# Low parts of streamed weight blocks on VectorE alone, in a two-layer decoder step with expert retrieval

## The chip, the cores and the metric

One core of a Trainium2 chip. Times are device microseconds of one execution of the whole program. PE is TensorE (PEld its weight loads), DVE is VectorE, ACT is ScalarE, POOL is GpSimd, SP is the engine that issues most DMAs here. L141 is line 141 of the kernel.

## What is computed

Two layers of a decoder for one prompt of 512 tokens and 8 sample sequences of 8 tokens: 576 tokens of 1024 channels, all in float32. A layer has a mixer (a gated linear recurrence and a short convolution) and then an expert retrieval, which is where the change lies:

```python
q = (xb @ w_q).reshape(tb, PEER_HEADS, 2, D_KEY_HALF)
s = jnp.einsum('thpd,hpkd->thpk', q, sub_keys).astype(jnp.float32)
sv, si = lax.top_k(s, TOPK)
cand = sv[:, :, 0, :, None] + sv[:, :, 1, None, :]
...
fv, fi = lax.top_k(cand, TOPK)
idx = jnp.take_along_axis(cand_idx, fi, axis=-1)
g = jax.nn.softmax(fv, axis=-1)
ue = u_tab[idx]
act = jax.nn.gelu(jnp.einsum('thkd,td->thk', ue, xb).astype(jnp.float32), approximate=False)
ve = v_tab[idx]
return jnp.einsum('thk,thkd->td', (g * act).astype(xb.dtype), ve)
```

8 heads choose 16 of 16384 experts for each token. An expert has a row of `u_tab`, whose product with the token is its activation, and a row of `v_tab`, which is added with weight gate times activation.

## The kernel before

**Two ways to the experts.** 384 tokens (TD) meet all 16384 experts on PE, 128 experts (a block) at a time; a gate matrix that is zero except at the chosen experts masks the result. For the other 192 tokens (three groups of 64, two partitions to a token) the chosen rows are gathered: 192 times a layer an indirect DMA, issued by GpSimd, brings one row of `u_tab` to each of 128 partitions (tile `ur`, L520), and VectorE forms the dot product with the token (L526); then 192 times a row of `v_tab` (`vr`, L520), which VectorE adds into `acc` (L541 the first time, L543 after). Between the two stand one Gelu over all dots and their product with the gates (`weigh`, L531). Five gathered tiles can be in flight (ROWS).

**Products in three passes.** Every streamed weight block [128, 1024] comes as `raw` (SP, L149; six in flight, RAWS) and is split in `split_blk` into `hi`, a rounded copy by ScalarE (L140), and `lo = raw - hi` (L141), a subtraction by VectorE or GpSimd; of each four can be in flight (HIS). PE multiplies hi with the high and the low part of the tokens, and lo with the high part. `turn` and `pool_share` say which engine makes lo: share 0 always VectorE (mixer), 0.5 every other block, 1.0 always GpSimd.

**The stages of the retrieval** of one layer:
- `queries`: 16 blocks of w_q (share 0.5), products pq (L722), scores, the 16 best of each half (`topk_half`, L586 to L591, on VectorE) and for the gathered tokens the choice of experts (`combine`, L601 to L661) and the dot steps as soon as their numbers are there.
- `dense_slots`: `combine` for the 384 tokens, four PE transposes (ptd, L771) for each 128.
- `phase_a`: 48 halves of gate pieces, each of two comparisons `oh` (L794) and two products `A` (L800) on VectorE, products pgm on PE (L805), a copy `stg` by ScalarE (L807) and, for two halves, a DMA to DRAM (gd, L809). Beside them the activations of the first 80 blocks of u: split (share SHARE_A = 1.0), product `pu` (L512, 24 matmuls a block), Gelu (L830).
- `phase_b`: for all 128 blocks the gates come back (gt, L886), activation times gate (L900), its split into wh and wl (L902, L903), the block of v (share SHARE_B = 0.5) and 18 matmuls `pvo` (L870). The last 48 blocks of u (names with `ub`, share SHARE_B) are multiplied here too, shortly before their v. pvo needs all gate pieces.

**What sets the order.** Nothing is ordered by hand. The program is written stage by stage, with the gathered steps strewn in by `pump` at rates QRATE, ARATE and BPUMP; a scheduler with a model of the engines' times then merges the instructions into one queue for each engine, by priority and by what it takes to be ready. Splits and loads of streamed blocks have a priority 2000 ahead (AHEAD). Each engine runs its queue strictly in that order.

Of the kernel before, what the change touches and what calls it, by code (L numbers as in the profile page):

```python
# [20 lines left out]
P = 128  # L21
L = 2              # layers
D = 1024
KT = D // P        # channel tiles
NP = 512           # prompt tokens
SB, ST = 8, 8      # sample sequences, steps
NS = SB * ST
T = NP + NS        # all tokens, prompt first
HA = 256           # the products over all tokens go by two parts, split here
# [4 lines left out]
TD = 384           # tokens that meet every expert on the tensor engine  # L34
NT = TD // P
NG = (T - TD) // 64  # groups of 64 tokens whose experts are gathered
NA = 80            # expert blocks that meet the tokens while the gates are formed
NS_ = NA - 16       # of these, the ones whose activations wait in DRAM
GI = 8             # expert blocks per reload
NCH = TD // 16     # 16-token pieces of the gate matrix  # L40
EPS = 1e-6
NEG = -3.0e38
GS = 16384.0       # keeps both float16 parts of a gate out of the subnormals
# [3 lines left out]
ROWSETS = [(0, 1), (1, 2), (2, 3), (3, 4), (4, 5), (5, 8), (8, 16)]  # rows of one length  # L47
AHEAD = 2000       # how far the streamed weights are put before the rest
NB = 4             # modulation chunks of the second layer that wait until the second norm of the first
NOW = 0            # the scheduler's rank of what the gathers and gates wait for  # L50
TROW = 1           # the pair of query blocks after which the gathered tokens' rows are formed
PACE = 0.8         # part of the first activations during which the gates are formed
TCOL = [0, 128, 384]    # tokens that meet every expert: first of each 128
GCOL = [256, 320, 512]  # tokens whose experts are gathered: first of each 64
NAT = 18           # gate pieces up to which every other one is formed where later activations stay
ONPE = (0, 256)    # tokens from these columns on have their squares summed on the tensor engine
SQ = 4             # pairs of blocks before the end at which the square root's table comes
WB = 2             # weighted activations in flight
X1, X2, X3 = 2, 3, 5   # modulation chunks before the load of x, its squares and its norm
EARLY = 20000      # how far the first loads are put before the rest  # L60
BOTH = 5           # modulation chunks in flight at the start
UAHEAD = 1         # pairs of blocks whose activations run ahead of their products
RAWS, HIS = 6, 4   # blocks of streamed weights in flight, as they come and split
ROWS = 5           # gathered rows in flight
SHARE_A, SHARE_B = 1.0, 0.5   # of the splits, what GpSimd takes
QRATE, ARATE, BPUMP = 0.3, 0.5, 1.6   # gathers issued beside queries, gates and products

# columns of the packed vectors
# [4 lines left out]
def hybrid_step(ctx: ExitStack, tc: tile.TileContext, xT, cT, wada, vecs, fnorm, win, wout, wq, subk,  # L73
# [18 lines left out]
    # ---------------------------------------------------------------- constants  # L92
# [25 lines left out]
    # conditioning vectors, one column quarter of the tensor engine wide, and the matrix that sums the four quarters  # L118
# [8 lines left out]
    # ---------------------------------------------------------------- helpers  # L127
    turn = [0.0]

    def split_blk(raw, nm, pool_share=0.0):  # L130
        """raw = hi + lo, both exact in float32r"""
        hi = st.tile([P, D], F32R, tag="hi", bufs=HIS, name=f"hi_{nm}")
        lo = st.tile([P, D], F32R, tag="lo", bufs=HIS, name=f"lo_{nm}")
        turn[0] += pool_share
        e = V
        if turn[0] >= 1.0:
            turn[0] -= 1.0
            e = G
        with tc.high_priority(offset=AHEAD):
            S.activation(hi, raw, AF.Copy)  # L140
            e.tensor_tensor(out=lo, in0=raw, in1=hi.bitcast(F32), op=ALU.subtract)  # L141
        return hi, lo

    def load_pair(src, nm, ahead=AHEAD):
        """two blocks of a stream, [P, D] each"""
# [6 lines left out]
    def mm_tokens(out, hi, lo, xh, xl, halves=((0, 1),)):  # L152
        """out[m, token] over all tokens, float32 from three passes"""
# [11 lines left out]
    def whole(o):  # L165
        """all tokens of a product in two banks"""
        return o.rearrange("p q t -> p (q t)")[:, 512 - HA:512 + HB]

# [4 lines left out]
    def ada(l, chunks, pool=None):  # L173
        """mod[p, part * 8 + k, sequence], 256 columns to a chunk. Four channel tiles at once go through the tensor
        engine, each in a column quarter of its own"""
# [23 lines left out]
    def bring(l, ch, n, ms):  # L199
        """n chunks' way to the partitions, with the bias"""  # L200
# [8 lines left out]
    def settle():  # L209
        """what was put off behind other work: the last chunk's way to the partitions, the last sums of the samples"""  # L210
        while late:
            late.pop()()

    def squares(pool, tag, k, c0, c1, nm):
        """ss += the squares of channel tile k"""
# [7 lines left out]
    def all_squares(c0, n, sq):  # L223
        """the squares of all channel tiles for n tokens, summed when rstd asks for them"""
# [8 lines left out]
    def rstd(c0, c1, nm):  # L233
        """ss = 1 / sqrt(mean square + eps)"""
# [12 lines left out]
    def norm_mod(pool, mod, nrm, part, nm, put, put_samples, ranges, tag=("nt", 2), ready=False):  # L247
        """modulate(rmsnorm(x)): shift at mod part, scale at part + 1. The prompt goes to put without the shift,
        channel tile by channel tile, the samples go whole and complete to put_samples"""
# [27 lines left out]
    def split_shift(hi, lo, tmp, shift):  # L277
        """tmp + shift = hi + lo"""
# [7 lines left out]
    def decay_rates():  # L286
        """-8 softplus(-lambda) and half of its size, the log1p by its atanh series"""
# [19 lines left out]
    # ---------------------------------------------------------------- mixer  # L307
    def mixer(l, vt, mod):
        with tc.tile_pool(name=f"hn{l}", bufs=1) as hn, tc.tile_pool(name=f"mh{l}", bufs=1) as mh:
# [6 lines left out]
            # output projection and residual  # L316
            g1 = mod[:, 2 * KT:3 * KT, :]
            for pr in range(KT // 2):
# [4 lines left out]
                # the last two by parts, so that the norm of the first part runs beside the second  # L323
# [18 lines left out]
    def mixer_in(l, vt, mod, mx, hnh, hnl, mgh, mgl):  # L342
# [25 lines left out]
        for c in range(KT):  # L368
# [22 lines left out]
            # recurrent branch: xa, its convolution, the gates, the scan  # L391
# [52 lines left out]
            # gated short convolution  # L444
# [34 lines left out]
    # ---------------------------------------------------------------- expert retrieval  # L479
    def peer(l, vt, mod):  # L480
# [4 lines left out]
        with tc.tile_pool(name=f"pg{l}", bufs=1) as pg:  # L485
            h2h = pg.tile([P, KT, TD], F32R, name="h2h")
            h2l = pg.tile([P, KT, TD], F32R, name="h2l")
            # slots of a gathered token: partition half r has heads 4 r + 0 .. 3
# [9 lines left out]
            def pump(n):  # L498
                """issue n more steps of the gathered tokens' work"""
# [16 lines left out]
            # tokens whose experts are gathered  # L516
# [67 lines left out]
    def topk_half(pool, sv, si, sc, nm, tick):  # L584
        """the 16 largest of the 128 scores and their places"""
# [8 lines left out]
    def combine(pool, sv4, si4, nh, nm, gate, ii, jj, tick, gscale=None, bufs=1):  # L594
        """the best 16 sums of each head: gates and both key numbers. Of the 256 sums (a, b) of the sorted halves
        only those with (a + 1)(b + 1) <= 16 can be among them; they lie row after row, row a from OFF[a] on"""
# [18 lines left out]
        # softmax over the 16  # L615
# [4 lines left out]
        # places: row a by comparison with the rows' starts, b = place - OFF[a]  # L620
# [12 lines left out]
        def rows(out):  # L633
            """out = the sums of pr's rows (integers up to 2048: exact)"""
# [28 lines left out]
    def queries(l, vt, mod, pg, pq, h2h, h2l, svd, sid, gidx, gate, xt, udot, gtasks, pump):  # L663
        """second norm, queries, scores, the best 16 keys of each half, and the gathered tokens' experts"""
# [28 lines left out]
        def token_rows():  # L693
            """the gathered tokens' vectors, token on the partition, in both halves"""
# [11 lines left out]
        for m in range(8):  # L706
# [6 lines left out]
            for u in range(2):  # L713
                hp = m + 8 * u
                hi, lo = split_blk(raw[u], f"wq{l}_{hp}", 0.5)
# [42 lines left out]
    def dense_slots(l, pk, svd, sid, sl, pump):  # L758
        """the chosen experts of the dense tokens, slots on the partition: both key numbers and the gate in two parts"""
# [14 lines left out]
    def phase_a(l, pg, pc, pa, sl, gd, ad, u_mm, pump):  # L774
        """gates as matrices to DRAM, and the activations of the first experts"""
# [3 lines left out]
        def slot(t, a, c0):  # L779
            """row a of the slots' numbers and gates for 8 tokens, beside every key number"""  # L780
            return sl[t][:, a, c0:c0 + 8].rearrange("p (g n) -> p g n", n=2).unsqueeze(2).to_broadcast([P, 4, P, 2])

        def gate_piece(t, ch):
            # pieces on their way to DRAM, the first ones also where later activations stay
# [32 lines left out]
        for pr in range(NA // 2):  # L817
# [8 lines left out]
            for u in range(2):  # L826
                i = 2 * pr + u
                hi, lo = split_blk(raw[u], f"u{l}_{i}", SHARE_A)
# [15 lines left out]
    def phase_b(l, pg, pc, pb, g2, gd, ad, res, u_mm, pump, finish):  # L844
# [9 lines left out]
        def meet(pair):  # L854
            """the activations of two blocks that come only now"""
# [3 lines left out]
            for u in range(2):  # L859
                i = i0 + 2 * pr + u  # L860
                hi, lo = split_blk(uraw[u], f"ub{l}_{i}", SHARE_B)
# [14 lines left out]
        for n, (i0, pr) in enumerate(pairs):  # L876
# [3 lines left out]
            if n == P // 2 - SQ:  # L880
                # brings the function's table early
# [12 lines left out]
            for u in range(2):  # L894
                i = i0 + 2 * pr + u
                w = acts[(i0, pr)][:, u, :] if at is None else at[:, i - i0, :]
                vh, vl = split_blk(vraw[u], f"v{l}_{i}", SHARE_B)
# [35 lines left out]
    # ---------------------------------------------------------------- the step  # L933
# [37 lines left out]
def _chan(a):  # L971
    """(..., D) -> channel-major (128, 8, ...)"""
# [5 lines left out]
def _layout(i):  # L978
# [7 lines left out]

    def pm(v, lead=()):  # (L, D) -> (L, P, KT)
        return v.reshape(L, -1, P).transpose(0, 2, 1)
# [5 lines left out]
    # column blocks in the order in which the mixer takes them: xa, ga, gb, cg, xs, bg  # L994
# [4 lines left out]
    w = i["peer_w_q"].reshape(L, KT, P, 2, 8, P).transpose(0, 4, 2, 3, 1, 5)  # l m p u k n  # L999
    o["wq"] = f(w.reshape(L, 8, P, 2, D))  # L1000
    o["subk"] = f(i["peer_sub_keys"].reshape(L, 2, 8, P, P).transpose(0, 2, 4, 1, 3))  # l m d u key
# [39 lines left out]
```

## Time and profile before

| | us |
|---|---|
| runs shown | 3847.15, 3849.39, 3852.28 |
| their median | 3849.39 |
| profiled execution, span from first to last instruction | 3846.9 |
| PE busy | 3484.8 |
| DVE busy | 3204.7 |
| POOL busy | 2022.2 |
| ACT busy | 1476.0 |

The profiled execution has no time of its own in the list of runs; its span is 0.3 us below the fastest run and 2.5 us below the median, so what lies around the span is no more than some microseconds. Layer 0 takes the first 1967 us, of which the retrieval is about 517 to 1945; layer 1 repeats it some 1870 us later. Busy time of an engine that is not waited for costs nothing, so the stretches are to be read one by one. An instruction's duration on DVE holds also the time in which it is held up after it has begun.

### The profile page before, as it was taken

To read this page: it belongs to the slowest core of one execution; us is meant where nothing else is said; L and a number is where in the kernel's file an instruction comes from. 1 tells how busy PE (TensorE), PEld (TensorE's weight loads), DVE (VectorE), ACT (ScalarE), POOL (GpSimd) and SP (SyncE) were. 2 spreads that over 40 slices of the span, in tenths; PEclk is the share of its full clock that TensorE was granted. 3 is DMA by queue.
4 is the path that set the end of the run, shared out by engine and by line. 5 is a ranking of instruction groups with operands and counts; after the bars stand their busy time and mean duration, and the time that the engine had idled before them with its cause. 6 is when DMAs were issued, how large, how long until landed. Compare 5 with 4: busy or idle time off the path is not lost.

```text
span 3846.9 us, 57240 instructions
## 1 busy us (share of the span) xinstructions
PE 3484.8 (91%) x21120; PEld 3180.7 (83%) x21120; DVE 3204.7 (83%) x5485; ACT 1476.0 (38%) x1876; POOL 2022.2 (53%) x1360
## 2 busy tenths in 40 slices
PE   8999998776879999999989998987677899999997
PEld 6999988776768999888879998877676799998886
DVE  5444489999997999998875556999999879999888
ACT  4444332322554333333344543222245533333332
POOL 1000037677536788776620002566764568887664
PEclk9999999888979999999989999988898899999998
DMA  6555237776878999999832221677678799999995
GB/s 249 188 189 165 69 138 263 246 233 223 291 272 298 334 338 340 341 358 362 315 131 79 82 83 65 209 254 233 225 263 279 280 338 322 338 357 342 355 341 200
DMA packets 366712, 960.62 MB, mean 250 GB/s; under 512 B 45920, under 2 KB 149472, under 8 KB 359648
## 3 DMA queue, kind: packets, MB, share of 16 engines
q1 hardware_dynamic: 239712, 478.77, 36.8%
q0 software_dynamic: 110592, 402.70, 30.0%
q10 hardware_dynamic: 16128, 75.50, 5.1%
q8 instruction: 165, 2.70, 0.3%
q14 instruction: 115, 0.94, 0.1%
HBM read 878.51 MB, written 78.30 MB: 249 GB/s over the span
## 4 chain that ended last, share of the span: by engine, by line
PE 55%; DVE 36%; issue 4%; DMA 2%; POOL 2%; ACT 1%; SPq 0%; DVEq 0%; POOLq 0%; ACTq 0%
PE pvo L870 19%; PE pj L159 16%; PE pu L512 12%; DVE ur L526 11%; DVE oh L794 4%; DVE A L800 4%; PE po L159 3%; POOL vr L520 1%; PE pq L722 1%; PE pm L189 1%; POOL lo_v L141 1%; DVE acc L543 1%; PE pg L420 1%; DMA raw_v<-in_vtab_dram 1%; PE pt L203 1%
## 5 line engine op out<-in xcount | busy, mean ns | idle before, releaser
L520 POOL DMA_INDIRECT ur<-in_utab_dram,gidx x384 | 481.6, 1254 | 512.9 <-DVE dot L526 281.2
L520 POOL DMA_INDIRECT vr<-in_vtab_dram,gidx x384 | 540.8, 1408 | 250.5 <-DVE acc L543 173.4
L543 DVE SCALAR_TENSOR_TENSOR acc<-vr,dot,acc 128x1024 f32<-128x1024 f32 x378 | 644.6, 1705 | 10.6 <-DMA vr<-in_vtab_dram,gidx 7.2
L526 DVE CUSTOM_DVE_ANT_0 ur<-ur,xt 128x1024 f32<-128x1024 f32 x384 | 613.4, 1605 | 8.8 <-DMA ur<-in_utab_dram,gidx 8.8
L512 PE MATMUL pu<-h2h,hi_u 128*128 128x384 f32 x1280 | 454.0, 355 | 62.4 <-ACT ao L830 62.4
L870 PE MATMUL pvo<-hi_v,wh 128*128 128x512 f32 x1536 | 488.7, 392 | 0.0
L870 PE MATMUL pvo<-lo_v,wh 128*128 128x512 f32 x1536 | 477.6, 390 | 0.0
L870 PE MATMUL pvo<-hi_v,wl 128*128 128x512 f32 x1536 | 466.0, 390 | 2.4 <-DVE acc L543 1.2
L512 PE MATMUL pu<-h2h,lo_u 128*128 128x384 f32 x1280 | 452.5, 353 | 6.0 <-POOL lo_u L141 5.9
L512 PE MATMUL pu<-h2l,hi_u 128*128 128x384 f32 x1280 | 451.2, 352 | 0.0
L141 POOL TENSOR_TENSOR lo_u<-raw_u,hi_u 128x1024 fp32r<-128x1024 f32 x160 | 405.6, 2537 | 28.5 <-ACT hi_u L140 25.7
L141 POOL TENSOR_TENSOR lo_v<-raw_v,hi_v 128x1024 fp32r<-128x1024 f32 x128 | 343.8, 2686 | 65.4 <-ACT hi_v L140 63.0
L159 PE MATMUL pj<-hnl,hi_wi 128*128 128x256 f32 (+1 forms) x1536 | 343.1, 301 | 2.5 <-DVE hnl L280 2.4
L159 PE MATMUL pj<-hnh,hi_wi 128*128 128x256 f32 (+1 forms) x1536 | 339.7, 301 | 5.5 <-ACT hnh L283 4.1
L870 PEld LDWEIGHTS pvo<-hi_v,wl 128*128 128x128 f32 x1536 | 288.1, 188 | 64.2 <-DVE wl L903 1.6
L870 PEld LDWEIGHTS pvo<-lo_v,wh 128*128 128x128 f32 x1536 | 288.3, 188 | 61.3
L159 PE MATMUL pj<-hnh,lo_wi 128*128 128x256 f32 (+1 forms) x1536 | 337.7, 298 | 0.0
L870 PEld LDWEIGHTS pvo<-hi_v,wh 128*128 128x128 f32 x1536 | 285.3, 188 | 54.9 <-issue 0.4
L512 PEld LDWEIGHTS pu<-h2h,hi_u 128*128 128x128 f32 x1280 | 256.4, 200 | 65.6 <-ACT ao L830 64.9
L140 ACT ACTIVATE hi_u<-raw_u 128x1024 fp32r<-128x1024 f32 x160 | 169.7, 1061 | 317.0 <-PE pu L512 162.4
L140 ACT ACTIVATE hi_v<-raw_v 128x1024 fp32r<-128x1024 f32 x256 | 272.0, 1062 | 29.5 <-issue 13.8
L512 PEld LDWEIGHTS pu<-h2h,lo_u 128*128 128x128 f32 x1280 | 255.9, 200 | 17.9 <-POOL lo_u L141 13.8
(319 smaller groups left out, 7592.8 us busy)
## 6 DMA issues: line engine op xcount, KB each, us to landing
raw_v<-in_vtab_dram SPq DMA_DIRECT2D x256, 512.0 KB
raw_u<-in_uT_dram SPq DMA_DIRECT2D x160, 512.0 KB
raw_wi<-in_win_dram SPq DMA_DIRECT2D x96, 512.0 KB
gd<-stg ACTq DMA_DIRECT2D x48, 1024.0 KB
raw_ub<-in_uT_dram SPq DMA_DIRECT2D x96, 512.0 KB
gt<-gd SPq DMA_DIRECT2D x768, 64.0 KB
raw_ada<-in_wada_dram SPq DMA_DIRECT2D x86, 512.0 KB
ad<-ao ACTq DMA_DIRECT2D x64, 384.0 KB
```

The costliest lines, as they stand in the source:

```text
L140: S.activation(hi, raw, AF.Copy)
L141: e.tensor_tensor(out=lo, in0=raw, in1=hi.bitcast(F32), op=ALU.subtract)
L159: PE.matmul(part(out, q), a[:, w], b[:, k, PARTS[q][0]:PARTS[q][1]], start=(k == 0 and a is hi and b is xh), stop=(k == KT - 1 and a is lo))
L189: PE.matmul(pm[j * 32:(j + 1) * 32, 0:256], c32[:, k, :], raw[k // 4][:, j * 256:(j + 1) * 256], start=(k < 4), stop=(k >= 4))
L203: PE.matmul(pt[:, q * 16:q * 16 + NSEQ], ms[:, q * P:(q + 1) * P], sel, start=True, stop=True)
L512: PE.matmul(pu[:, 0:TD], a[:, w], b[:, k, 0:TD], start=(k == 0 and a is hi and b is h2h), stop=(k == KT - 1 and a is lo))
L520: G.indirect_dma_start(out=rt, out_offset=None, in_=tab, in_offset=bass.IndirectOffsetOnAxis(ap=gidx[:, g, h, k:k + 1], axis=0))
L526: V.tensor_tensor_reduce(out=ur, in0=ur, in1=xt[g], scale=1.0, scalar=0.0, op0=ALU.mult, op1=ALU.add, accum_out=dot[:, g, h, k:k + 1])
L543: V.scalar_tensor_tensor(out=acc[g], in0=vr, scalar=w, in1=acc[g], op0=ALU.mult, op1=ALU.add)
L794: V.tensor_tensor(out=o, in0=iota2.unsqueeze(1).to_broadcast([P, 4, P, 2]), in1=slot(t, a, c0), op=ALU.is_equal)
L800: V.tensor_tensor(out=A[:, z], in0=oh[0], in1=slot(t, 2 + z, c0), op=ALU.mult)
L870: PE.matmul(pv[t][q], a[:, tk], b[:, q * 512:(q + 1) * 512], start=(n == 0 and a is wh and b is vh), stop=(n == P - 1 and a is wl))
```

## The change

GpSimd's share becomes 0 in all four places where blocks are split with a share: the 16 blocks of w_q, and the u and v blocks of phase_a and phase_b. `split_blk` itself stays. The rest of the diff drops comments.

```diff
-SHARE_A, SHARE_B = 1.0, 0.5   # of the splits, what GpSimd takes
+SHARE = 0.0
...
-                hi, lo = split_blk(raw[u], f"wq{l}_{hp}", 0.5)
+                hi, lo = split_blk(raw[u], f"wq{l}_{hp}", SHARE)
...
-                hi, lo = split_blk(raw[u], f"u{l}_{i}", SHARE_A)
+                hi, lo = split_blk(raw[u], f"u{l}_{i}", SHARE)
...
-                hi, lo = split_blk(uraw[u], f"ub{l}_{i}", SHARE_B)
+                hi, lo = split_blk(uraw[u], f"ub{l}_{i}", SHARE)
...
-                vh, vl = split_blk(vraw[u], f"v{l}_{i}", SHARE_B)
+                vh, vl = split_blk(vraw[u], f"v{l}_{i}", SHARE)
```

The scheduler makes other queues of it. Three places follow, before and after; numbers behind a name are block or step and a tile's number.

VectorE in `dense_slots` of layer 0, around the cast of the first gates (L766); before:

```order
L526 ISA ur_1_1_14_9148,dot_4954<-ur_1_1_14_9148,xt_1_5521 128x1024
L526 ISA dot_4954 128x1
L766 CAST ghd_0_7090<-ggd_0_7088 128x128
L637 TENSOR_TENSOR t8d_0_7170<-t8d_0_7170 128x128x2
L613 MAX_INDEX fid_1_7235<-fvd_1_7234,c2d_1_3_7259 128x8
L611 MATCH_REPLACE c2d_1_4_7265<-fvd_1_7234,candd_1_7226 128x50
```

and after:

```order
L141 TENSOR_TENSOR lo_u_62_10970<-raw_u_31_10964,hi_u_62_10969 128x1024
L526 ISA ur_1_2_0_11870,dot_4954<-ur_1_2_0_11870,xt_1_5521 128x1024
L526 ISA dot_4954 128x1
L766 CAST ghd_0_7090<-ggd_0_7088 128x128
L613 MAX_INDEX fid_1_7235<-fvd_1_7234,c2d_1_2_7253 128x8
L637 TENSOR_TENSOR t8d_0_7170<-t8d_0_7170 128x128x2
L141 TENSOR_TENSOR lo_u_63_11000<-raw_u_31_10965,hi_u_63_10999 128x1024
L613 MAX_INDEX fid_1_7235<-fvd_1_7234,c2d_1_3_7259 128x8
L526 ISA ur_1_2_1_11900,dot_4954<-ur_1_2_1_11900,xt_1_5521 128x1024
```

Subtractions have come into VectorE's queue, the block of u beside the same cast is 63, and the dot steps have gone on from the second to the third head of their group.

VectorE in the gate stage of layer 0; before:

```order
L794 TENSOR_TENSOR oh_1_32_9014<-iota_83,sl_1_4956 128x1024
L794 TENSOR_TENSOR oh_1_32_9016<-iota_83,sl_1_4956 128x1024
L800 TENSOR_TENSOR A_1_32_9021<-oh_1_32_9014,sl_1_4956 128x1024 x2
L526 ISA ur_1_2_10_12294,dot_4954<-ur_1_2_10_12294,xt_1_5521 128x1024
L526 ISA dot_4954 128x1
L794 TENSOR_TENSOR oh_1_40_9042<-iota_83,sl_1_4956 128x1024
L794 TENSOR_TENSOR oh_1_40_9047<-iota_83,sl_1_4956 128x1024
L800 TENSOR_TENSOR A_1_40_9049<-oh_1_40_9042,sl_1_4956 128x1024 x2
```

and after:

```order
L543 SCALAR_TENSOR_TENSOR acc_0_15106<-vr_0_2_3_15906,dot_4954,acc_0_15106 128x1024
L794 TENSOR_TENSOR oh_1_40_9047<-iota_83,sl_1_4956 128x1024
L800 TENSOR_TENSOR A_1_32_9021<-oh_1_32_9014,sl_1_4956 128x1024 x2
L543 SCALAR_TENSOR_TENSOR acc_0_15106<-vr_0_2_4_15936,dot_4954,acc_0_15106 128x1024
L794 TENSOR_TENSOR oh_1_40_9042<-iota_83,sl_1_4956 128x1024
L543 SCALAR_TENSOR_TENSOR acc_0_15106<-vr_0_2_5_15970,dot_4954,acc_0_15106 128x1024
L794 TENSOR_TENSOR oh_1_48_9143<-iota_83,sl_1_4956 128x1024
L800 TENSOR_TENSOR A_1_40_9049<-oh_1_40_9042,sl_1_4956 128x1024 x2
```

The gathered work beside the same gate products was the 43rd dot of the second group; now all dots are done and the sums of the first group run.

PE at the last gate product of layer 0 (pgm); before:

```order
L805 LDWEIGHTS oh_2_120_10938
L805 MATMUL pgm_2_7_1_10932<-A_2_120_10940,oh_2_120_10938 128x128
L512 MATMUL pu_73_11326<-h2l,hi_u_73_11322 128x384
L512 MATMUL pu_73_11326<-h2h,lo_u_73_11323 128x384
L512 MATMUL pu_73_11326<-h2h,hi_u_73_11322 128x384
```

and after:

```order
L805 LDWEIGHTS oh_2_120_10938
L805 MATMUL pgm_2_7_1_10932<-A_2_120_10940,oh_2_120_10938 128x128
L512 MATMUL pu_82_11626<-h2h,hi_ub_82_11622 128x384
L512 MATMUL pu_82_11626<-h2l,hi_ub_82_11622 128x384
L512 MATMUL pu_82_11626<-h2h,lo_ub_82_11623 128x384
```

In both the first pvo stands behind pu of block 85, or two matmuls into it, so PE has 283 matmuls of pu between the two before and 96 after.

## Rows read from the trace of the kernel before

**Rows 1.** The page: busy time of each engine, and the chain that ended last.

```profile
PE 3484.8 (91%) x21120; PEld 3180.7 (83%) x21120; DVE 3204.7 (83%) x5485; ACT 1476.0 (38%) x1876; POOL 2022.2 (53%) x1360
PE 55%; DVE 36%; issue 4%; DMA 2%; POOL 2%; ACT 1%; SPq 0%; DVEq 0%; POOLq 0%; ACTq 0%
```

**Rows 2.** Table by stretch: start:end, length, engines' busy time, granted clock, DMA share, GB/s.

```profile
core 0: us, PE busy (x) PEld busy (x) DVE busy (x) ACT busy (x) POOL busy (x), PEclk, DMA share, GB/s
517.00:1186.00 669.00, 527.11 (x3478) 497.85 (x3477) 655.38 (x1605) 247.83 (x273) 392.49 (x233) 0.88 0.72 243
1186.00:1945.00 759.00, 757.76 (x3672) 665.57 (x3670) 674.59 (x644) 285.49 (x378) 567.24 (x325) 1.00 0.95 338
...
960.00:1190.00 230.00, 176.88 (x1352) 159.08 (x1351) 229.24 (x289) 126.38 (x98) 116.32 (x71) 0.86 0.81 281
1335.00:1596.00 261.00, 261.00 (x1330) 238.57 (x1329) 248.94 (x201) 94.01 (x127) 215.29 (x122) 1.00 0.95 342
```

**Rows 3.** Tiles A (layer 0), ur, oh, lo_u, lo_wi: duration min/median/max, first and last start.

```profile
L800 DVE TENSOR_TENSOR A<-oh,sl x96: 675/682/3261, 968.0 to 1182.0; 128x1024 f16<-128x1024 f16 x96
L526 DVE CUSTOM_DVE_ANT_0 ur<-ur,xt x384: 1192/1212/4065, 569.7 to 3198.4; 128x1024 f32<-128x1024 f32 x192
L794 DVE TENSOR_TENSOR oh<-iota,sl x192: 674/681/5640, 960.0 to 3052.1; 128x1024 f16<-128x1024 f16 x192
L141 POOL TENSOR_TENSOR lo_u<-raw_u,hi_u x160: 2346/2407/4423, 618.9 to 3069.7; 128x1024 fp32r<-128x1024 f32 x160
L141 DVE TENSOR_TENSOR lo_wi<-raw_wi,hi_wi x96: 1197/1224/1226, 36.2 to 2274.9; 128x1024 fp32r<-128x1024 f32 x96
```

**Rows 4.** The chain that ended last: the gate stage (first line), then 1186 to 1345 us.

```profile
by line: DVE oh L794 33.9%; DVE A L800 31.0%; DVE ur L526 24.7%; PE pu L512 7.3%; PE pgm L805 2.0%; issue 1.3%; DVE dot L526 0.2%
by line: PE pu L512 63.3%; PE pvo L870 36.3%; PE pgm L805 0.6%; issue 0.0%
1186.88 49.14 PE pu L512 x283
...
1248.42 8.20 PE pvo L870 x36
1256.62 8.34 PE pu L512 x48
```

**Rows 5.** Groups of DVE, 517 to 1186 us: busy, mean ns, idle before, releasers.

```profile
L526 DVE CUSTOM_DVE_ANT_0 ur<-ur,xt 128x1024 f32<-128x1024 f32 x147 | 235.9, 1606 | 4.8 <-DMA ur<-in_utab_dram,gidx 4.8
L794 DVE TENSOR_TENSOR oh<-iota,sl 128x1024 f16<-128x1024 f16 x96 | 85.5, 921 | 0.3
L800 DVE TENSOR_TENSOR A<-oh,sl 128x1024 f16<-128x1024 f16 x96 | 82.6, 900 | 0.5
```

**Rows 6.** Timeline of DVE in three places: start, length, instruction.

```profile
1186.37 1.21 DVE L526 CUSTOM_DVE_ANT_0 ur<-ur,xt 128x1024 f32<-128x1024 f32 x1
1187.51 1.21 DVE L526 CUSTOM_DVE_ANT_0 ur<-ur,xt 128x1024 f32<-128x1024 f32 x1
1188.66 3.42 DVE L526 CUSTOM_DVE_ANT_0 ur<-ur,xt 128x1024 f32<-128x1024 f32 x1
...
1238.79 1.21 DVE L141 TENSOR_TENSOR lo_v<-raw_v,hi_v 128x1024 fp32r<-128x1024 f32 x1
1239.93 0.54 DVE L900 TENSOR_TENSOR ao<-ao,gt 128x384 f32<-128x384 f32 x1
...
1606.33 1.27 DVE L543 SCALAR_TENSOR_TENSOR acc<-vr,dot,acc 128x1024 f32<-128x1024 f32 x1
1607.53 1.21 DVE L141 TENSOR_TENSOR lo_v<-raw_v,hi_v 128x1024 fp32r<-128x1024 f32 x1
```

**Rows 7.** Groups of POOL, 517 to 1186 us.

```profile
L141 POOL TENSOR_TENSOR lo_u<-raw_u,hi_u 128x1024 fp32r<-128x1024 f32 x76 | 193.1, 2543 | 14.3 <-ACT hi_u L140 13.0
L141 POOL TENSOR_TENSOR lo_wq<-raw_wq,hi_wq 128x1024 fp32r<-128x1024 f32 x6 | 14.6, 2432 | 38.2 <-ACT hi_wq L140 38.2
```

**Rows 8.** Groups of DVE and POOL in the gate stage, 960 to 1190 us.

```profile
L526 DVE CUSTOM_DVE_ANT_0 ur<-ur,xt 128x1024 f32<-128x1024 f32 x49 | 74.0, 1515 | 0.0
L141 POOL TENSOR_TENSOR lo_u<-raw_u,hi_u 128x1024 fp32r<-128x1024 f32 x25 | 62.9, 2518 | 12.2 <-ACT hi_u L140 11.8
```

**Rows 9.** The page: the queue of the 768 gathers.

```profile
q0 software_dynamic: 110592, 402.70, 30.0%
```

**Rows 10.** Timeline of ACT, SP, DVE from A to B; of PE and DVE at layer 0's end.

```profile
1189.95 0.33 ACTq L809 DMA_DIRECT2D gd<-stg  x1
...
1206.23 4.62 SPq L886 DMA_DIRECT2D gt<-gd  x7
...
1233.07 3.71 DVE L900 TENSOR_TENSOR ao<-ao,gt 128x384 f32<-128x384 f32 x4 [2.38 <-DMA gt<-gd]
...
1944.34 1.03 PE L920 MATMUL pyt<-ident,ys 128*128 128x128 f32 x8
...
1961.16 1.19 DVE L543 SCALAR_TENSOR_TENSOR acc<-vr,dot,acc 128x1024 f32<-128x1024 f32 x1
```

## The prediction

> **What bounds the kernel now.** I read the page first, then its stages one by one. The page says that PE is busy 91% and DVE 83% of the span, and that the chain that ended last is 55% PE and 36% DVE [rows 1]: two different bounds, so the next view is the table by stretch, here for the expert retrieval of the first layer (the second layer repeats it). From 517 to 1186 us DVE is busy 655 of 669 us while PE works 527; from 1186 to 1945 us PE is busy 758 of 759 and the DMA engines stand at 0.95 with 338 GB/s [rows 2]. I call the first stretch A (queries, gates; its last gate product on DVE starts at 1182.0 [rows 3]) and the second B (all expert products). The chain agrees: in the gate stage DVE's oh, A and ur make up 90% of it, after it pu and pvo of PE do [rows 4]. So **a microsecond of DVE work counts if it stands ahead of the last A, and counts nothing behind it**; for PE it is the other way round.
>
> In A DVE is not simply working. A dot step (L526) has a median of 1212 ns and a mean of 1606, an oh product 681 and 921, an A product 682 and 900 [rows 3, 5]. The timeline shows why: a dot that takes 1.21 us among its neighbours takes 3.42 once [rows 6], about its own time plus one GpSimd subtraction (2407 ns [rows 3]). The mixer, where GpSimd does no subtraction, has lo_wi on DVE at 1197 to 1226 ns with no tail [rows 3].
>
> **What the change removes.** All 352 subtractions of GpSimd. In A these are 76 lo_u and 6 lo_wq [rows 7]. What one costs DVE: in the gate stage 49 dots are 303 ns over the median, 96 oh 240, 96 A 218 [rows 5, 8]: 14.8 + 23.0 + 20.9 = 59 us on 25 subtractions, 2.36 us each. With 76 x 2.36 = 179 us for lo_u, where DVE never idles, and 0 to 14 us for lo_wq, where part of DVE's 13.6 idle us lies, I take **-185 us** in A of one layer. The ends: 102 us, which the three large groups of A show alone (147 x 394 + 96 x 240 + 96 x 218 ns), and 193.
> The Trainium skill (SBUF — State Buffer, Who interferes with whom) says that a DVE instruction with two SBUF inputs and a GpSimd one that reads SBUF exclude each other for the whole instruction. By that each of the 82 would cost up to its mean of 2.54 us, 208 us, and the forecast would fall by 23 us a layer; the row's 2.36 decides.
>
> **What it adds to A.** A subtraction on DVE: from start to start 1.14 us (1238.79 to 1239.93 [rows 6]). The order has 94 of them on DVE between the first score of the top-16 search and the last A, where it had 5: 89 x 1.14 = **+101.5 us**. Had only this happened, A would shrink by 83 us.
>
> **What it moves.** The order is a scheduler's, and without subtractions in GpSimd's queue it puts the gathered work much earlier. Counted in the order up to the last A of a layer: dots 146 before, 192 now; weighted sums (L543, L541) 0 before, 92 now, one between nearly every two gate instructions. These lay in B, where DVE had 84 us to spare (675 busy of 759 [rows 2]); now they stand in a queue that runs in order, ahead of the work that opens B. A dot is 1.15 us from start to start (1186.37 to 1187.51), a sum 1.20 (1606.33 to 1607.53) [rows 6]: 46 x 1.15 + 92 x 1.20 = 52.9 + 110.4 = **+163.3 us**. A's DVE work so changes by -185 + 101.5 + 163.3 = **+80 us**; by the ends of the lock +72 to +163.
>
> **New waits in A.** Three things now run close together. (a) DMA: A moved 243 GB/s x 669 us = 163 MB; 138 more gathers of 0.524 MB (402.70 MB by 768 [rows 9]) make 235 MB. B shows what the chip gives when asked for all, 338 GB/s, 342 in its middle [rows 2]: 690 to 695 us, under the 749 of DVE, but in stretches with dots close together (32 in 50 us of DVE work) the demand is 335 to 355 GB/s, and DVE waits for a late gather in order. (b) PE: the order now has 1584 products of pu ahead of the first transpose of the gates, 877 before; at 49.14 us for 283 [rows 4], 0.174 each, that is 275 us beside about 285 us of DVE work, through hi and lo buffers four deep (HIS). A subtraction on DVE that finds its hi buffer held by PE stops the dots, search and gate steps queued behind it; on GpSimd only gathers stood behind it. (c) ScalarE's Gelu ahead of the first sum, a new wait in the gate stage. At least 0; at most 90 us, if A fell to the 281 GB/s of the gate stage (235 MB, 836 us). I take **+30 us** (4% of A), nearer the low end, because the waits for gathers shown are small: 4.8 us in A [rows 5].
>
> **B.** PE's work behind the last A: 283 pu products ran ahead of the first pvo, 96 do now; 1030 stood behind it, 1008 now. 2304 pvo at 8.20 us for 36 are 524.8 us, 1008 pu 175 us [rows 4]: 700 us. The 283 had hidden 49 us of a delay: last stg, gd to DRAM (issued at 1189.95), 24 gt loads from 1206.23 on, the first multiplication with gt at 1233.07 [rows 10]. Now 96 hide 17 us of it. On SP the gt loads now stand behind six stream blocks more (up to the first raw_v of 80_2), and on DVE 6 subtractions and 16 sums stand between the last A and that multiplication, 6 x 1.14 + 16 x 1.20 = 26 us, where 4 and 14 dots did. I take 30 us from the last A to the first pvo, between 28 (these and the multiplications) and the 50 of before. So PE idles some 13 us, a wait that was hidden. B: 759 before, 30 + 700 + 4 (before's last pvo, right ahead of the transpose at 1944.34 [rows 10], is later than 1186 + 50 + 179 + 525 by as much) = 734, **-25 us** (-27 to -5). That DVE has less to do in B, and DMA less to carry (72 MB), is worth nothing while PE is the bound there. The end of a layer, where sums ran until 1962 behind the last pvo [rows 10], can gain 0 to 10 us; I take 0, since the transposes and squares follow the last pvo in any case. The mixer keeps its subtractions: 0 within 3 us.
>
> **Sum.** A layer: 80 + 30 - 25 = +85 us; two layers +170. The profiled execution has a span of 3846.9 us; 3846.9 + 170 = 4017 us, on the median of the runs (2.5 us higher) 4019. I say **4018 us**. What a measurement of this kernel can tell from no change is about 0.2%, 8 us.
>
> **Rivals.**
> - *Faster: the lock is all that counts.* If the dots and sums moved ahead of the last A cost nothing there, A would shrink by 83 us a layer. PE could follow (it idles 142 us in A) and B would lose no more than above, so 3847 - 2 x 83 - 2 x 25 = 3631 us, and about 3681 if B kept its length. For: the price of the lock is the best shown number here. Against: DVE takes its queue in order, the gates' last product stands behind those 138 steps, and A had no idle time to hold them. It decides where DVE's work ahead of the last A comes to less than 669 + 25 = 694 us; the sum is 749, so 55 us would have to be missing, a dot or a sum at less than two thirds of its clean price. Chance 0.04.
>   The Trainium skill (GPSIMD Engine Reference, Engine selection) would have elementwise work go to VectorE, GpSimd being about twice as slow; 2543 against 1212 ns [rows 3, 7] bears the ratio out. By that rule alone this rival would be the forecast; it weighs one instruction, not what the scheduler does with the engine set free.
> - *Much slower: A turns into a DMA or PE bound.* At 281 GB/s, A takes 836 us, +167 a layer: 2 x (167 - 25) = +284, 4131 us. For: demand at the level of B's ceiling, three resources within 10%. Against: B ran at 338 to 342 GB/s for 759 us with PE never waiting. Chance 0.15.
> - *No change:* the two effects cancel, if the clean work inserted is overstated and the lock understated, each by about 40 us. Chance 0.03.
> - *The change does not do what it says:* the order has no L141 on GpSimd any more, 352 before. Excluded.
>
> **How the numbers follow.** The forecast's case has 0.78: its own range, with waits of 0 to 90 us, B at -27 to -5 and the lock at its ends, runs from about 3940 to 4340 if all ends fell together, most of it within 3950 and 4110. Leaving out the faster rival and the outer half of the very slow one gives 3930 to 4130 us. Faster by over 0.2%: 0.04; within: 0.03; slower: 0.93.
>
> **What would show it.** Right: no POOL group of L141; medians and means of dots, oh and A equal within 50 ns; oh, A and acc side by side in the gate stage; the last A of layer 0 near 1295 us instead of 1182; GB/s of A above 290 and of B below 270; PE idle 10 to 15 us ahead of the first pvo, then B in about 734 us. Waits of DVE for gathers or hi_u in A well over 30 us would show the second rival. Wrong: a last A before 1205 us, or dots and sums shorter than 1.1 us.

## The result, and the profile after

| | before | after |
|---|---|---|
| median of four runs each (range), us | 3850.06 (3847.15 to 3852.28) | 4029.84 (4026.36 to 4033.70) |
| ratio after to before, 95% interval | | 1.0468 [1.0453, 1.0483] |
| span of the profiled execution, us | 3846.9 | 4025.1 |

The kernel has become 4.7% slower, 180 us; the forecast was 4018 us, about 170 more than before. The profiled execution after took 4027.04 us, 1.9 us more than its span.

The page of after, busy time and the chain that ended last, which answers to [rows 1]:

```profile
PE 3453.8 (86%) x21120; PEld 3156.0 (78%) x21120; DVE 2948.8 (73%) x5837; ACT 1473.1 (37%) x1876; POOL 1192.1 (30%) x1008
PE 75%; DVE 7%; issue 6%; DMA 6%; POOL 5%; ACT 1%; SPq 0%; POOLq 0%; DVEq 0%; ACTq 0%
```

DVE has 352 instructions more than before and is busy 256 us **less**; GpSimd has 352 fewer. No engine is busy longer than it was, and yet the kernel is slower. The page alone cannot explain that, and its chain even points away: DVE's share falls from 36 to 7%. The stretches show where the time went. The table by stretch of after, with its borders just behind the last gate product and the last pvo of layer 0, which answers to the first two lines of [rows 2]:

```profile
517.00:1289.00 772.00, 545.22 (x3663) 518.83 (x3662) 743.94 (x1871) 262.98 (x289) 424.29 (x290) 0.81 0.87 310
1289.00:2036.00 747.00, 722.86 (x3462) 630.56 (x3461) 463.05 (x546) 268.38 (x358) 121.93 (x94) 0.98 0.73 242
```

In A DVE is busy 744 of 772 us where it was 655 of 669: 89 us more. In B it is busy 463 us where it was 675. Work of DVE has moved from the stretch where PE is the bound to the one where DVE is. Groups of DVE in A, from 517 to 1289 us, against [rows 5]:

```profile
L526 DVE CUSTOM_DVE_ANT_0 ur<-ur,xt 128x1024 f32<-128x1024 f32 x192 | 231.9, 1220 | 14.5 <-DMA ur<-in_utab_dram,gidx 11.4 <-issue 2.3
L543 DVE SCALAR_TENSOR_TENSOR acc<-vr,dot,acc 128x1024 f32<-128x1024 f32 x91 | 117.2, 1288 | 1.4 <-DMA vr<-in_vtab_dram,gidx 1.4
L141 DVE TENSOR_TENSOR lo_u<-raw_u,hi_u 128x1024 fp32r<-128x1024 f32 x80 | 97.6, 1220 | 2.8 <-ACT hi_u L140 2.7
L794 DVE TENSOR_TENSOR oh<-iota,sl 128x1024 f16<-128x1024 f16 x96 | 66.5, 694 | 0.0
L800 DVE TENSOR_TENSOR A<-oh,sl 128x1024 f16<-128x1024 f16 x96 | 62.2, 694 | 0.0
```

One dot costs 1220 ns on average instead of 1606, an oh 694 instead of 921, an A 694 instead of 900: the long instructions are gone. The 192 dots now cost less than the 147 did (231.9 against 235.9 us). But 91 sums (117 us) and 80 lo_u (98 us) stand there that A did not have. The timeline of DVE in the gate stage shows how the sums lie, one between nearly every two gate products:

```profile
1150.41 1.28 DVE L543 SCALAR_TENSOR_TENSOR acc<-vr,dot,acc 128x1024 f32<-128x1024 f32 x1
1151.60 0.69 DVE L794 TENSOR_TENSOR oh<-iota,sl 128x1024 f16<-128x1024 f16 x1
1152.20 1.29 DVE L800 TENSOR_TENSOR A<-oh,sl 128x1024 f16<-128x1024 f16 x2
1153.41 1.28 DVE L543 SCALAR_TENSOR_TENSOR acc<-vr,dot,acc 128x1024 f32<-128x1024 f32 x1
1154.60 0.69 DVE L794 TENSOR_TENSOR oh<-iota,sl 128x1024 f16<-128x1024 f16 x1
1155.20 1.29 DVE L543 SCALAR_TENSOR_TENSOR acc<-vr,dot,acc 128x1024 f32<-128x1024 f32 x1
```

Of the 4.79 us from 1150.41 to 1155.20 two sums take 1.19 and 1.19 from start to start. The chain is no guide here: from 1031 to 1289 us it goes 31% through GpSimd's issuing of `vr` and 27% through pu, and 3% through oh and A, but DVE is busy 251 of these 258 us (the table by stretch at the end), so nothing that it waits for can be worth more than 7. Tile A of layer 0 (duration min/median/max, first and last start), against the first line of [rows 3]:

```profile
L800 DVE TENSOR_TENSOR A<-oh,sl x96: 678/692/719, 1033.6 to 1285.1; 128x1024 f16<-128x1024 f16 x96
```

The last gate product starts at 1285.1 us instead of 1182.0, 103.1 later. From there the layer is quicker than before: the last pvo starts 750.8 us behind it (2035.9), where it was 762.1 (1944.1). The first product of the next mixer starts at 2053.2, 86.9 us later than before (1966.3). The second layer repeats it: last A 190.0 us later than before (3243.3), last pvo 182.7 later (3995.3), last instruction 178.2 later.

### The profile page after: what moved, and what is told of

Same layout as the page of the kernel before. It is cut to its first block, busy times and chain, and to the rows that moved or that the text cites. A ratio compares the mean times of both kernels' runs of the same rounds, so it can differ in the third digit from the quotient of the medians.

```text
span 4025.1 us, 57158 instructions
## 1 busy us (share of the span) xinstructions
PE 3453.8 (86%) x21120; PEld 3156.0 (78%) x21120; DVE 2948.8 (73%) x5837; ACT 1473.1 (37%) x1876; POOL 1192.1 (30%) x1008
## 4 chain that ended last, share of the span: by engine, by line
PE 75%; DVE 7%; issue 6%; DMA 6%; POOL 5%; ACT 1%; SPq 0%; POOLq 0%; DVEq 0%; ACTq 0%
PE pvo L870 26%; PE pu L512 25%; PE pj L159 15%; POOL vr L520 4%; PE po L159 3%; DMA ur<-in_utab_dram,gidx 2%; PE pq L722 2%; POOL ur L520 2%; DVE ur L526 1%; PE pm L189 1%; DMA vr<-in_vtab_dram,gidx 1%; PE pg L420 1%; DMA gt<-gd 1%; PE pgm L805 1%; PE pt L203 1%
## 5 line engine op out<-in xcount | busy, mean ns | idle before, releaser
L520 POOL DMA_INDIRECT vr<-in_vtab_dram,gidx x384 | 589.3, 1535 | 425.1 <-DVE acc L543 381.4
L520 POOL DMA_INDIRECT ur<-in_utab_dram,gidx x384 | 509.0, 1326 | 552.6 <-DVE dot L526 152.4
L543 DVE SCALAR_TENSOR_TENSOR acc<-vr,dot,acc 128x1024 f32<-128x1024 f32 x378 | 485.9, 1286 | 14.9 <-DMA vr<-in_vtab_dram,gidx 13.6
L526 DVE CUSTOM_DVE_ANT_0 ur<-ur,xt 128x1024 f32<-128x1024 f32 x384 | 463.5, 1219 | 28.6 <-DMA ur<-in_utab_dram,gidx 25.4
L512 PE MATMUL pu<-h2h,hi_u 128*128 128x384 f32 x1280 | 432.4, 338 | 6.7 <-ACT at L830 4.7
L512 PE MATMUL pu<-h2h,lo_u 128*128 128x384 f32 x1280 | 431.2, 337 | 6.5 <-DVE lo_u L141 6.5
L141 DVE TENSOR_TENSOR lo_v<-raw_v,hi_v 128x1024 fp32r<-128x1024 f32 x256 | 313.3, 1224 | 88.1 <-ACT hi_v L140 83.0
L805 PE MATMUL pgm<-A,oh 128*128 128x128 f16 x1536 | 174.9, 281 | 215.2 <-DVE A L800 215.2
L805 PEld LDWEIGHTS <-oh 128*128 128x128 f16 x1536 | 138.3, 127 | 251.9 <-DVE A L800 188.9
L807 ACT ACTIVATE stg<-pgm 128x1024 f32<-128x1024 f32 x96 | 187.7, 1960 | 251.8 <-PE pgm L805 218.6
```

The lines of the kernel that those rows point to most:

```text
L512: PE.matmul(pu[:, 0:TD], a[:, w], b[:, k, 0:TD], start=(k == 0 and a is hi and b is h2h), stop=(k == KT - 1 and a is lo))
L520: G.indirect_dma_start(out=rt, out_offset=None, in_=tab, in_offset=bass.IndirectOffsetOnAxis(ap=gidx[:, g, h, k:k + 1], axis=0))
L526: V.tensor_tensor_reduce(out=ur, in0=ur, in1=xt[g], scale=1.0, scalar=0.0, op0=ALU.mult, op1=ALU.add, accum_out=dot[:, g, h, k:k + 1])
L543: V.scalar_tensor_tensor(out=acc[g], in0=vr, scalar=w, in1=acc[g], op0=ALU.mult, op1=ALU.add)
L805: PE.matmul(o, oh[1][:, n // 2, :, n % 2], A[:, z, n // 2, :, n % 2], start=(z == 0), stop=(z == 1))
L807: S.activation(stg[:, :, half * 8:half * 8 + 8].rearrange("p i t -> p t i"), pgm.rearrange("p q (t i) -> p (q t) i", i=P), AF.Copy, scale= ...
```

## The experiments

In these batches the kernel before has a median of 3849.43 us (for the three changed kernels that hold work back, and the change in B alone) or 3850.16 (for the others). "Order" is the count in VectorE's queue up to the last A of a layer; after has 192 dots, 92 sums and 94 subtractions there.

**The sums held back by half.** The theory: it is the gathered work ahead of the last A that costs, at its clean price. The rival: the loss is PE or DMA, or subtractions on DVE are dear in themselves. The scheduler takes what is ready, so a real dependency is put in: a zero is made from a gate product and given to the Gelu as bias, which leaves its value as it is. With PIECE_V = 12 the Gelu, and the sums behind it, wait for the 13th of 24 gate pieces. BPUMP, the rate at which B's part of the program takes gathered steps, goes from 1.6 to 1.9 in all kernels with such a dependency.

```diff
-                S.activation(dot, dot, AF.Gelu)
+                S.activation(dot, dot, AF.Gelu, bias=zero["v"])
...
-                after_u()
+                held.append((PIECE_V, lambda A: V.tensor_scalar(out=zero["v"], in0=A, scalar1=0.0, scalar2=None, op0=ALU.mult)))
+                held.append((PIECE_V, lambda A: after_u()))
...
             S.dma_start(gd[t * 8 + ch], stg)
+            while held and held[0][0] <= t * 8 + ch:
+                held.pop(0)[1](A[:, 1, 3, P - 1, 0:1])
```

> The changed kernel with one more dependency: the Gelu of the dots waits for the 13th of 24 gate pieces, so the order has 42 weighted sums ahead of the last gate product where the changed kernel has 92; dots (192), subtractions (94) and PE's order around the gates are the same. Theory (a gathered step ahead of the last gate product costs its own time): 50 x 1.20 = 60 us a layer less, 4030 - 120 = 3910 us, the last A of layer 0 near 1226 us. Rival (the subtractions in VectorE's queue, tied to PE by the hi buffers, make the time, and the sums only fill its gaps): within 20 us of 4030.

Measured: 3916.64 us, ratio to before 1.0174 [1.0157, 1.0191]. Against after that is -113 us, 57 a layer, for 50 sums fewer in A: 1.13 us each, while PE's pu products between the last gate product and the first pvo (96) and behind it (1008) stayed as in after.

**The sums held back altogether.** The same with the last piece:

```diff
-PIECE_U, PIECE_V = None, 12
+PIECE_U, PIECE_V = None, 23
```

> As above with the Gelu behind the last gate piece: no sum ahead of the last gate product, 192 dots, 85 subtractions; 254 products of pu between the last gate product and the first pvo (96 in the changed kernel) and 1080 behind (1008). Theory: in A 92 x 1.20 + 9 x 1.14 = 120 us a layer less; in B 230 more pu, 40 us, less the 22 us for which PE waited ahead of the first pvo: 102 us a layer, 4030 - 204 = 3826 us, below the kernel before. Rival: 4010 to 4030 us.

Measured: 3817.23 us, ratio 0.9918 [0.9902, 0.9935]. With no sum ahead of the last A the change is already a gain.

**The fourth head's dots held back too.** Its 48 dots get their expert numbers only from the last gate piece, as the numbers plus the same kind of zero:

```diff
-PIECE_U, PIECE_V = None, 23
+PIECE_U, PIECE_V = 23, 23
...
+                        def release(A, last=last):
+                            V.tensor_scalar(out=zero["u"], in0=A, scalar1=0.0, scalar2=None, op0=ALU.mult)
+                            V.tensor_scalar(out=gidx[:, :, 3, :], in0=last, scalar1=zero["u"], scalar2=None, op0=ALU.add)
+                            gtasks.extend([lambda g=g, k=k: udot(g, 3, k) for g in range(NG) for k in range(16)])
```

> As hold_v, and the numbers of the fourth head's experts are released only at the last gate piece too: 144 dots and no sum ahead of the last gate product, about the 146 and 0 of the kernel before, with all subtractions on VectorE. Theory: 48 x 1.15 = 55 us a layer less again, 3826 - 110 = 3716 us, if B stays PE's (its DMA then asks for about 335 GB/s, as before the change); the price of the lock shows as the difference to the kernel before, some 65 us a layer. Rival: not below 3850 us, since the subtractions stay where they are.

Measured: 3702.86 us, ratio 0.9617 [0.9600, 0.9633]: faster than both kernels, by 327 us against after, with every low part still formed on VectorE. The page of this kernel, its table by stretch, and the chain of its gate stage (980 to 1112 us; L815 and L809 are A and oh here):

```profile
PE 3438.1 (93%) x21120; PEld 3147.5 (85%) x21120; DVE 2948.1 (80%) x5843; ACT 1472.8 (40%) x1876; POOL 1114.3 (30%) x1008
PE 82%; DVE 11%; DMA 3%; issue 2%; ACT 1%; POOL 1%; SPq 0%; ACTq 0%; DVEq 0%; POOLq 0%
```

```profile
517.00:1115.00 598.00, 503.03 (x3466) 479.28 (x3465) 571.09 (x1676) 250.29 (x271) 193.59 (x145) 0.89 0.73 266
1115.00:1880.00 765.00, 761.39 (x3675) 668.98 (x3673) 634.35 (x751) 283.14 (x380) 320.41 (x239) 1.00 0.96 342
```

```profile
by line: DVE A L815 32.4%; DVE oh L809 30.4%; PE pu L515 22.1%; PE pgm L820 9.1%; ACT stg L822 3.0%; issue 1.7%; ACT L847 1.0%; ACT at L847 0.4%; ACTq L824 0.2%; ACTq L822 0.0%
```

DVE's total busy time is that of after within a microsecond (2948.1 against 2948.8 us). The same work in another order is worth 327 us. In the chain of the gate stage the dots, a quarter of it before [rows 4], are gone; the sums and dots stand in B again, where DVE is busy 634 of 765 us and PE 761.

**The two dependencies without the change.** The same edits in the kernel before, to see whether they do something by themselves.

> Control for hold_uv: the same two dependencies put into the kernel before, with its shares for GpSimd kept. The order up to the last gate product has 144 dots, no sums, 5 subtractions on VectorE; pu 241 and 1080 around the first pvo, as in hold_uv (254 and 1080). Theory: as the kernel before, 3850 us within 15, so that hold_uv against this is the place of the subtractions alone, about 73 us a layer. Rival (the dependencies themselves make hold_uv fast): 3700 to 3760 us.

Measured: 3849.17 us, ratio 0.9996 [0.9986, 1.0005]. They cost and bring nothing there. So this pair, before with the dependencies and the change with them, differs in who subtracts while the gathered work stays behind the gates in both: 3849.17 to 3702.86, -146 us, -73 a layer.

**The lock taken away, the order kept.** In the kernel before GpSimd's subtraction becomes a memset of lo, which reads nothing; GpSimd keeps an instruction in that place, and VectorE keeps its queue. (The lock is what the prediction calls it when a GpSimd subtraction holds up an instruction of VectorE.)

```diff
-            e.tensor_tensor(out=lo, in0=raw, in1=hi.bitcast(F32), op=ALU.subtract)
+            if e is G:
+                G.memset(lo.bitcast(F32), 0.0)
+            else:
+                V.tensor_tensor(out=lo, in0=raw, in1=hi.bitcast(F32), op=ALU.subtract)
```

> The kernel before with each subtraction of GpSimd replaced by a memset of the same tile, which reads nothing; the low parts of those 352 blocks are left out. The order up to the last gate product is as before (146 dots, no sums, 5 subtractions). Theory (a GpSimd instruction that reads SBUF holds up VectorE): the means of dots, oh and A fall to their medians, VectorE has 185 us less in A; A is then near what PE needs (527 of 669 us before), so I expect 110 to 140 us a layer less, 3570 to 3630 us. Rival (the long instructions of VectorE come from the gathers or DMA traffic): 3820 to 3860 us, means unchanged.

Measured: 3525.84 us, ratio 0.9165 [0.9138, 0.9192], more of a gain than the 3570 to 3630 expected. The table by stretch of A, and DVE's and POOL's groups in it (L529 is the dot, L797 oh, L803 A):

```profile
517.00:1030.00 513.00, 485.41 (x3450) 464.34 (x3449) 486.14 (x1594) 249.48 (x271) 263.43 (x235) 0.96 0.87 316
```

```profile
L529 DVE CUSTOM_DVE_ANT_0 ur<-ur,xt 128x1024 f32<-128x1024 f32 x151 | 182.8, 1215 | 8.5 <-DMA ur<-in_utab_dram,gidx 8.5
L797 DVE TENSOR_TENSOR oh<-iota,sl 128x1024 f16<-128x1024 f16 x96 | 63.0, 687 | 9.6 <-PE pgm L808 5.8 <-PE ptd L774 3.1 <-issue 0.4
L803 DVE TENSOR_TENSOR A<-oh,sl 128x1024 f16<-128x1024 f16 x96 | 61.9, 686 | 0.4
...
L142 POOL MEMSET lo_u<- 128x1024 f32 x77 | 74.4, 968 | 49.1 <-PE pu L515 49.0
```

The tail of the durations goes when the subtraction goes, with a GpSimd instruction of 968 ns in its place, and the last A of layer 0 starts at 1021.8 us, 160.2 sooner; the layer gains 162 (324 for two), all of it. The Trainium skill (SBUF — State Buffer, Who interferes with whom) says that a VectorE instruction with two SBUF inputs contends with a GpSimd one that reads SBUF, not with one that only writes it; these rows agree (1215 ns beside memsets, 1606 beside subtractions). A memset does still hold up a few casts: two of pfg (L630) took 1227 and 1802 ns, where after (L627) these take at most 190.

This gives the price of a subtraction that GpSimd makes. The table by stretch from 517 us to the last A of layer 0, of memset and then of before:

```profile
517.00:1022.00 505.00, 477.41 (x3382) 456.49 (x3381) 479.91 (x1584) 241.94 (x265) 259.40 (x232) 0.96 0.87 317
517.00:1182.00 665.00, 523.11 (x3446) 494.17 (x3444) 651.38 (x1603) 246.25 (x271) 389.76 (x232) 0.88 0.72 242
```

DVE is busy 479.9 us here and 651.4 in the kernel before, with the same 146 dots: 171.5 us less for 82 GpSimd instructions [rows 7], 2.09 us each. (Some 4 us of it are 19 short instructions of the search that run ahead of 517 us here.)

**The change in one stretch alone.** Before with share 0 only in `phase_b` (SHARE_Q, SHARE_A, SHARE_B = 0.5, 1.0, 0.0), and only ahead of it (0.0, 0.0, 0.5).

> The kernel before with only the blocks of phase_b (ub and v) split by VectorE alone; its order up to the last gate product is as before (146 dots, no sums, 5 subtractions). Theory (B is PE's bound): no change, 3850 us within 10, although GpSimd no longer holds up VectorE in B. A theory by which the lock counts everywhere would see up to 60 us a layer less; one by which subtractions in VectorE's queue hold up PE would see more than 3860.

> The kernel before with only w_q and the u blocks of phase_a split by VectorE alone; ub and v as before. The order has 192 dots, 92 sums and 92 subtractions ahead of the last gate product, as the changed kernel. Theory: the whole loss is here; phase_b's part was worth -10 us by itself, so 4030 to 4050 us. Rival (some of the loss comes from B): 3930 to 4010 us.

Measured: 3840.32 us, ratio 0.9975 [0.9965, 0.9985], for B alone; 4025.47 us, ratio 1.0462 [1.0444, 1.0479], for A alone. The whole loss lies in A. The change in A alone comes out 4.5 us below the 4030 to 4050 expected: B's part takes 9 us off the kernel before, but added to A's part it brings nothing (4029.84 with both). With B alone, the last A starts at 1183.4 us, as before, and the second stretch reads:

```profile
1186.00:1945.00 759.00, 758.82 (x3680) 666.91 (x3678) 629.81 (x736) 284.18 (x380) 318.01 (x238) 1.00 0.96 340
```

45 us less of DVE there than in [rows 2] (674.59), for a program that is 5 us a layer quicker: PE stays busy through all of it. Where these 5 us come from stays open.

All together, by what stands on DVE ahead of the last A of layer 0:

| kernel | dots, sums, subtractions | DVE busy from 517 us to the last A, us | last A starts, us | time, us |
|---|---|---|---|---|
| after | 192, 92, 94 | 741 | 1285.1 | 4029.84 |
| sums from piece 13 on | 192, 42, 94 | 684 | 1229.9 | 3916.64 |
| sums behind the gates | 192, 0, 85 | 624 | 1167.6 | 3817.23 |
| fourth head's dots too | 144, 0, 85 | 569 | 1111.3 | 3702.86 |
| before, with the dependencies | 144, 0, 5 | 649 | 1181.4 | 3849.17 |
| before, memset for the subtraction | 146, 0, 5 | 480 | 1021.8 | 3525.84 |

(The counts of the fourth and fifth row are from the trace, the others from the order.) In every row DVE's busy time fills the stretch up to the last A but for 15 to 30 us. From the first row to the second 50 sums move the last A by 55.2 us, 1.10 each; from the third to the fourth 48 dots move it by 56.3, 1.17 each. Those are the prices of the prediction (1.20 and 1.15) within 0.1 us.

## Why the prediction was right

The sign and the mechanism hold: 4029.84 us against 4018. The size holds too, but in part by luck: three terms were off by 13 to 17 us a layer, and these errors offset to 2. The terms, for one layer:

- **The lock, -185 us: mis-sized by 13.** It measured -171.5 (2.09 us a subtraction instead of 2.36), within the ends 102 and 193. The 2.36 came from the gate stage [rows 5, 8], where one large two-input instruction of DVE follows another. Elsewhere a subtraction costs less, as the trace of before shows instruction by instruction. Of the 81 subtractions that start in A, 77 overlap exactly one lengthened instruction of DVE (over 150 ns above the usual time of its form); the lengthening is 2.35 us for each subtraction in the gate stage, and 2.13 from 620 to 960 us. In that stretch DVE also runs the search, and the search's own instructions are not lengthened (none of the 360 of L586 to L591 in A took over 295 ns; two rows of before follow); that a subtraction passes in part beside them would explain the difference, and is not shown by itself.

```profile
L591 DVE FIND_INDEX8 sid<-svd,s2d 128x8 uint32<-128x128 f32 x48 | 13.3, 281 | 0.0
L590 DVE MAX8 svd<-s2d 128x8 f32<-128x128 f32 x48 | 12.6, 279 | 0.0
```

  After, without subtractions on GpSimd, they take 294 and 292 ns. The exclusive lock for the whole instruction, by which the prediction got 208 us from the Trainium skill (SBUF — State Buffer, Who interferes with whom), lies further off than the 185.
- **The subtractions on DVE, +101.5, and the dots and sums moved, +163.3: right.** With the lock as measured they make +93; DVE's busy time up to the last A rose by 90 (741 against 651). The table above confirms the prices of sums and dots one by one. Had only the subtractions moved, A would shrink, as the prediction says. The pair with the dependencies shows by how much: 80 subtractions come onto DVE there (85 against 5), so the terms make 171.5 - 80 x 1.14 = 80 us, and DVE's busy time falls by 80 (649 to 569). The last A comes only 70.1 us earlier (1181.4 to 1111.3), because DVE idles 26 us instead of 16.
- **New waits in A, +30: they came to 13.** DVE idles 27 us ahead of the last A (768 less 741) instead of 13.6. Of the three causes given, gathers came late for 11.4 us (4.8 before), lo_u waited 2.7 for hi_u, and the Gelu is in none of the rows. At 310 GB/s A drew less on average than the 338 that B shows [rows 2], but 338 to 342 is not what the chip gives when asked for all, as the prediction read it: one stretch of A drew 364.

```profile
700.00:815.00 115.00, 115.00 (x676) 114.71 (x675) 114.48 (x355) 46.94 (x66) 50.49 (x41) 1.00 0.97 364
```

- **B, -25: only -11.** The step that failed is "I take 30 us from the last A to the first pvo". It took 46.5 (1285.1 to 1331.6), near the upper of its two bounds (28 and 50), and PE idled 24.1 us there instead of 13. The rest of B was right: from the first pvo to the last it took 704.3 us, forecast 700 + 4. Why it is 46.5 shows in the chain of waits from 1285 us on:

```profile
1291.17 1.92 ACT stg L807
...
1293.11 9.54 DMA gd<-stg
...
1302.79 0.33 SPq L886
...
1306.07 6.46 DMA raw_v<-in_vtab_dram
...
1316.79 10.99 DMA gt<-gd
...
1327.81 2.66 DMA gt<-gd
...
1330.48 0.57 DVE ao L900
...
1331.07 0.53 ACT wh L902
```

The prediction priced this by what stood on DVE (26 us). But the path is one of transfers and of the queue that issues them: the last gates go to DRAM (9.5 us), and only then the reloads are issued, from 1302.79 on; the multiplication follows at 1330.48, 27.7 us later. Of these, 14.0 pass while SP issues reloads one by one, with blocks of u and v between them, and 13.7 in the last two transfers. Before, the same leg took 26.8 us (1206.23 to 1233.07 [rows 10]). The row for it was there, and the leg did not shrink when DVE's part did; the prediction had named SP's queue without giving it a price. What PE waited for, of after, from 900 to 1335 us:

```profile
PE pgm L805 <- DVE A L800: 105.8, 70, 5.8
PE ptd L771 <- DVE iid L638: 73.9, 2, 37.1
PE ptd L771 <- DVE jjd L638: 38.1, 3, 14.7
PE pvo L870 <- ACT wh L902: 24.1, 1, 24.1
```

- **The tail, 0: -5.** From the last pvo to the first product of the next mixer 17 us instead of 22 (its first pj starts at 2053.2, before at 1966.3), within the 0 to -10 allowed.

The errors offset: A with its waits came to +103 where the sum had 110, B to 14 us more than forecast, the tail to 5 less; that leaves 2 us a layer, 87 against 85.

The markers: no L141 on POOL; medians and means of dots, oh and A within 3 ns of each other; acc between the gate products; 310 and 242 GB/s in the two stretches; last A at 1285.1, forecast near 1295. All came but PE's idle time ahead of the first pvo and the 734 us of B.

The rivals. *Faster, the lock alone:* its mechanism is real and it fell on the order only. The version with the work held back is what it described, with B keeping its length: 3703 us where the rival said about 3681. The rule that the prediction named beside it, elementwise work on VectorE rather than GpSimd (the Trainium skill, GPSIMD Engine Reference, Engine selection), holds here once the order is held: 3849.17 to 3702.86 us. *Much slower, a DMA or PE bound in A:* fell, DVE waited for gathers 11.4 us in 772. It was near, though: from 610 to 912 us PE was busy for 297 of 302 us beside DVE's 296. *No change* fell with the measured prices.

## What to carry to other kernels

When an engine that issues transfers is relieved of work, ask what it will issue earlier, and on whose queue the work that depends on it then stands: a scheduler that takes what is ready fills the critical stage with work that a later stage had for nothing. Give each microsecond of moved work the price of the stage it lands in, not of the engine's total, and hold early work back with a real dependency if it lands in the wrong one. A duration whose mean lies far over its median can be a sign that another engine holds the instruction up, as it was here; a memset in the other's place then prices it.

## What the runs showed of the hardware

- PE sat idle for a whole stage after the change, at next to no cost. The table by stretch of after, `dense_slots`:

```profile
912.00:1031.00 119.00, 3.92 (x12) 2.00 (x12) 111.55 (x239) 3.20 (x6) 90.40 (x65) 0.51 0.86 290
1031.00:1289.00 258.00, 151.79 (x1132) 133.80 (x1133) 251.45 (x315) 114.58 (x81) 171.14 (x102) 0.65 0.93 328
```

PE had its products of u done early, then waited for DVE's slots (73.9 and 38.1 us ahead of ptd, above); the granted clock fell to 0.51, near the lower of its two levels (1.2 of 2.4 GHz), and was 0.65 on average through the gates. DVE was the bound there, so the time shows little of either: the first eight pvo take 3.55 us (1331.65 to 1335.20), where eight take 1.82 at full clock (8.20 for 36 [rows 4]).
- The reverse with memset: the matmuls of A that took 527 us at a clock of 0.88 [rows 2] took 485 us (3450 of them instead of 3478) at 0.96, while the gate products on PE waited 18.9 us for A instead of 53.0. PE's busy time in A was no floor at 527, so the gain came through whole.
- The indirect gathers that GpSimd issues do not lengthen DVE's two-input instructions in any way the rows show: the longest of the 384 dots of after took 1298 ns, of before 4065 [rows 3]:

```profile
L526 DVE CUSTOM_DVE_ANT_0 ur<-ur,xt x384: 1172/1219/1298, 570.2 to 2998.8; 128x1024 f32<-128x1024 f32 x192
```
